# A trunk step on one core: bias gather issued one head ahead, small fills on DVE, the last modulation rows drained two chunks sooner

## The chip, the core and the metric

The kernel runs on one core of a Trainium2 chip. The metric is the time of one execution in device microseconds; the time before is the median of three runs. Engines are named as in the profile: PE (matmuls; PEld its weight loads), DVE (vector), ACT (scalar), POOL (GpSimd), SP (issues most DMAs). All instructions of an engine run in their order, and a DMA that an engine issues stands in that order too.

## What is computed

One layer of a flow-matching trunk on 128 context tokens and 256 latent tokens, width 2048, in fp32. Per layer (cut from the reference):

```python
mod = silu(cond) @ w_mod + b_mod               # six vectors: sh1, sc1, g1, sh2, sc2, g2
h = rmsnorm(x, ln1_g) * (1 + sc1) + sh1
z = h @ w_in                                   # q, k, v, conv a, conv g, LRU x, LRU gate
att = softmax(q k^T * scale + na_bias) v       # 8 heads; window bias for latent tokens, cached context
cv  = silu(layernorm(dwconv31(a * sigmoid(g))))
rec = RG_LRU(dwconv4(x)) * gelu(gate)          # forward and backward scan
x = x + g1 * (concat(att, cv, rec) @ w_out)
h = rmsnorm(x, ln2_g) * (1 + sc2) + sh2
u = dwconv3(h @ ffn_up); ug, uv = split(u)
x = x + g2 * ((silu(ug) * uv) @ ffn_down)
y = rmsnorm(x, final_g)
```

Outputs are y for both token groups, the new keys and values of the context, and the last LRU states.

## The kernel before

Every large product is made of three passes over reduced-width halves (`mm3`, lines L164 to L166: high by high, high by low, low by high). Weights come from HBM by SP's DMAs into `raw`; ACT makes the high half `whi` (L151), DVE the low half `wlo` (L153). All 384 tokens (three row tiles of 128) pass through in one go.

The program runs through the stages: modulation of the first norm, `in_proj` (columns of conv and LRU), `qkv`, `out_proj`, `ffn`. While PE works through the large products of a stage, smaller work is woven in as generators ("streams"): after a number of products `st.turn` advances each stream by some of its yields, and the scheduler fixes each engine's order when the kernel is built. `st.drain(name)` runs what is left of a stream. The streams here are
- `recurrent` (L760 on): per chunk c of four, `lu` is filled with zeros on POOL (L768), then convolved; the two gates, the tails between the token groups set to zero on POOL (L807, L808), the state copied in on POOL (L811), the scans on DVE (L812, L815).
- `conv_module` (L714 on): `cu` filled on POOL (L719), and 31 DVE instructions per chunk (L723, L726) into `cacc`.
- `attention(h)` (L649 on) for each head: after `yield LAG0` it takes two bias tiles and calls `bias_tile`, which loads each in two DMAs on POOL's queue (L643) and masks each half with two selects on POOL (L645, L646). Then three score tiles: PE `S` (L665), DVE adds the bias and takes the maximum (L669 to L674), ACT exponentiates (L675), DVE takes the reciprocal (L676), ACT scales (L677). Then PE transposes the scaled scores into `PTp` (L686) and multiplies them by V (`o`, L695).
- `mods` and `modsd`: the modulation of the second half. Rows of `w_mod` (`rawm`) are loaded by SP for PE's own sums (L383, `modp`), or by POOL (L398) for sums on DVE (L405, L407 into `acc`), which PE gathers with `sel` (L413). `mod_cols` copies the result to M on ACT (L421), PE transposes M (`modt`, L424), DVE adds the bias into MC (L429).

`out_proj` makes five column chunks, `WO_COLS`, of 512, 512, 512, 256 and 256 columns; after each, the residual and its squares (L891, L894, L895) are made for each row tile. After the last chunk `mods` and `modsd` are drained, and the FFN begins with the scaled x (`xs`, L1039), its transposes (`xtp`, L483), `ht` on ACT (L489), `hh` and `hl` on DVE (L491, L492).

Of the kernel before, what the change touches and what calls it, by code (L numbers as in the profile page):

```python
# [18 lines left out]
NH = 8  # L19
# [6 lines left out]
CTX = 128  # L26
# [37 lines left out]
def flat_ap(ap, offset, dims):  # L64
    return bass.AP(tensor=ap.tensor, offset=ap.offset + offset, ap=dims)
# [35 lines left out]
class Trunk:  # L101
# [314 lines left out]
    def mod_cols(self, vec, slot, ln_g, rows):  # L416
        nc = self.nc
        pm = self.aux_ps("modp")
        yield from rows(vec, pm)
        M = self.misc("M")[:, :512]  # L420
        nc.scalar.copy(M, pm)  # L421
        pt = self.aux_ps("modt")
        for b in range(4):
            nc.tensor.transpose(out=pt[:, b * P:(b + 1) * P], in_=M[:, b * P:(b + 1) * P], identity=self.ident)  # L424
        for b in range(4):
            src = pt[:, b * P:(b + 1) * P].rearrange("p (j c) -> p j c", j=4)[:, :, 0:2]
            dst = self.MC[:, slot, b:KT:4, :]
            bm = self.bmod[:, vec * KT + b:(vec + 1) * KT:4]
            nc.vector.tensor_tensor(dst, src, bm.unsqueeze(2).broadcast_to([P, 4, 2]), ALU.add)  # L429
        if ln_g is not None:  # L430
            dst = self.MC[:, slot]
            nc.vector.scalar_tensor_tensor(dst, dst, 1.0, ln_g.unsqueeze(2).broadcast_to([P, KT, 2]), ALU.add, ALU.mult)
# [154 lines left out]
    def qkv(self):  # L587
        nc = self.nc
        h = self.h
        st = self.streams  # L590
        nc.gpsimd.dma_start(self.V[:, 3, :], self.I["cache_v"])

        def v(n):
            pv = [self.mm_ps() for _ in range(3)]
# [37 lines left out]
        qk(6)  # L632


    def bias_tile(self, h):
        nc = self.nc
        bts = [self.slot(LAT, "bias") for _ in range(2)]
        nb = self.I["na_bias"]
        for i in range(2):
            for r in range(2):  # L640
                v = bts[i][r * 64:(r + 1) * 64, :LAT].rearrange("p (k c) -> p k c", c=64)
                off = 3719 - (h * 465 + (10 - (2 * i + r)) * 31 + 15 + 63)
                nc.gpsimd.dma_start(v, flat_ap(nb, off, [[1, 64], [31, 4], [1, 64]]))  # L643
                lo, hi = v[:, :, 16:64], v[:, :, 0:48]
                nc.gpsimd.affine_select(lo, lo, [[0, 4], [-1, 48]], ALU.is_ge, NEG, base=55, channel_multiplier=-1)  # L645
                nc.gpsimd.affine_select(hi, hi, [[0, 4], [1, 48]], ALU.is_ge, NEG, base=-56, channel_multiplier=1)  # L646
        return bts

    def attention(self, h):  # L649
        nc = self.nc  # L650
        q, k = self.z[h], self.z[8 + h]
        yield LAG0
        bt = self.bias_tile(h)
        hs = slice(h * P, (h + 1) * P)
        PT = self.misc("PT")[:, :3 * LAT].rearrange("p (j q) -> p j q", j=3)
        PC = self.slot(P, "PC")
# [1 line left out]
        for i in range(3):  # L658
# [18 lines left out]
            nc.scalar.activation(s, s, AF.Copy, scale=st[:, 2:3])  # L677
            ss.append(s)
            yield 1.0
        yield LAG1  # L680
        for i in range(3):
            n = P if i == 0 else T
# [25 lines left out]
    def conv_module(self):  # L708
# [7 lines left out]
        for c in range(4):  # L716
            a, g = self.z[24 + c], self.z[28 + c]
            u = self.mp.tile([P, W], F32, tag="cu", bufs=2, name="cu")
            nc.gpsimd.memset(u, 0.0)  # L719
            nc.vector.tensor_tensor(u[:, 15:15 + CTX], a[:, :CTX], g[:, :CTX], ALU.mult)  # L720
            nc.vector.tensor_tensor(u[:, 30 + CTX:30 + T], a[:, CTX:], g[:, CTX:], ALU.mult)
            acc = self.slot(N, "cacc")
            nc.vector.tensor_scalar(acc, u[:, 0:N], self.cvw[:, c:c + 1], self.cv_b[:, c:c + 1], ALU.mult, ALU.add)  # L723
            yield 1.0
            for w in range(1, 31):
                nc.vector.scalar_tensor_tensor(acc, u[:, w:w + N], self.cvw[:, 4 * w + c:4 * w + c + 1], acc,  # L726
                                               ALU.mult, ALU.add)
                yield 0.5
            self.mark = nc.vector.tensor_copy(self.cmark, acc[:, 0:1])
            us.append(acc)  # L730
# [29 lines left out]
    def recurrent(self):  # L760
# [4 lines left out]
        for c in range(4):  # L765
            x = self.z[32 + c]
            u = self.mp.tile([P, TP + 3], F32, tag="cu", bufs=2, name="lu")
            nc.gpsimd.memset(u, 0.0)  # L768
            nc.scalar.copy(u[:, 2:2 + CTX], x[:, :CTX])
            nc.scalar.copy(u[:, 4 + CTX:4 + T], x[:, CTX:])  # L770
            xc = self.slot(TP, "xc")
# [30 lines left out]
            for d in range(2):  # L802
# [1 line left out]
                a, gi, r = av[d], gis[d], rs[d]  # L804
                nc.vector.scalar_tensor_tensor(r, a, 1.0, r, ALU.add, ALU.mult)
                nc.vector.tensor_tensor(gi, gi, r, ALU.mult)
                nc.gpsimd.memset(a[:, CTX:CTX + 2], 0.0)  # L807
                nc.gpsimd.memset(gi[:, CTX:CTX + 2], 0.0)  # L808
                st = self.st[:, m:m + 1]
                if d == 0:  # L810
                    nc.gpsimd.tensor_copy(gi[:, CTX + 1:CTX + 2], st)  # L811
                    nc.vector.tensor_tensor_scan(r, a, gi, 0.0, ALU.mult, ALU.add)  # L812
                    nc.vector.tensor_copy(lasts[:, m:m + 1], r[:, CTX - 1:CTX])
                else:
# [24 lines left out]
    def out_proj(self):  # L839
# [32 lines left out]
        for n, (c0, cw) in enumerate(WO_COLS):  # L872
            if n == nn - 1:
                self.ahead = [self.wchunk_slots(self.I["ffn_up"], 0, 4, b, 256) for b in (0, DFF)]
            if n == 0:
                pps = products((0, 1))
            elif n > 1:
                pps = products((n,))
# [17 lines left out]
            if n < 2:  # L896
                with tc.issue_after(ins.ins):
                    self.late_cols(GX, 1024 + n * 512)
        st.drain("mods")
        st.drain("modsd")  # L900
        return ssq

    def late_cols(self, G, c0, cw=512):
# [186 lines left out]
                yield 1.0  # L1090

    def run(self):
        self.mixf, self.gd = {}, {}
        self.setup()
        self.in_proj()
        st = self.streams
# [61 lines left out]
```

## Time and profile before

| | |
|---|---|
| median of three runs | 1807.93 us (1806.61 to 1808.3) |
| the profiled execution | 1806.54 us |
| its span | 1804.6 us |
| its mean granted clock of PE | 0.991 |
| PE busy | 1747.1 us, 97% of the span |
| DVE, ACT, POOL busy | 1158.5, 695.2, 144.9 us |

The profile's page gives each engine's busy time, the chain of work that ended last, and the costliest groups of instructions. The trace behind it answers for any stretch: the timeline of one engine (with the idle time before an instruction and what ended it, in brackets), the waits summed by kind, and busy time with the granted clock by window. All times are microseconds from the start of the span.

### The profile page before, as it was taken

To read this page: it belongs to the slowest core of one execution; us is meant where nothing else is said; L and a number is where in the kernel's file an instruction comes from. 1 tells how busy PE (TensorE), PEld (TensorE's weight loads), DVE (VectorE), ACT (ScalarE), POOL (GpSimd) and SP (SyncE) were. 2 spreads that over 40 slices of the span, in tenths; PEclk is the share of its full clock that TensorE was granted. 3 is DMA by queue.
4 is the path that set the end of the run, shared out by engine and by line. 5 is a ranking of instruction groups with operands and counts; after the bars stand their busy time and mean duration, and the time that the engine had idled before them with its cause. 6 is when DMAs were issued, how large, how long until landed. Compare 5 with 4: busy or idle time off the path is not lost.

```text
span 1804.6 us, 25289 instructions
## 1 busy us (share of the span) xinstructions
PE 1747.1 (97%) x9989; PEld 1579.2 (88%) x9989; DVE 1158.5 (64%) x1629; ACT 695.2 (39%) x1003; POOL 144.9 (8%) x279
## 2 busy tenths in 40 slices
PE   6999998898999999999999999999999999999998
PEld 5789986767987789998989999998989999898987
DVE  4599697795865976449654545449854545448467
ACT  5223455575444335334333333232323333233324
POOL 0100001112441110001000000001000000000002
PEclk9999999999999999999999999999999999999999
DMA  9988659788774864337534343437434343643432
GB/s 335 331 284 284 222 179 260 211 254 240 204 177 157 327 231 138 122 129 246 163 117 131 126 129 117 129 128 225 154 123 129 121 127 116 221 152 121 125 126 108
DMA packets 234551, 325.58 MB, mean 180 GB/s; under 512 B 12140, under 2 KB 169812, under 8 KB 233536
## 3 DMA queue, kind: packets, MB, share of 16 engines
q1 hardware_dynamic: 220976, 277.98, 47.2%
q0 software_dynamic: 13344, 45.94, 9.8%
q8 instruction: 78, 1.28, 0.3%
q14 instruction: 41, 0.34, 0.1%
q10 hardware_dynamic: 112, 0.05, 0.0%
HBM read 316.54 MB, written 7.38 MB: 179 GB/s over the span
## 4 chain that ended last, share of the span: by engine, by line
PE 84%; DVE 7%; DMA 4%; issue 2%; SPq 1%; ACT 1%; POOL 1%; DVEq 0%; POOLq 0%; ACTq 0%
PE mmp L166 26%; PE mmp L165 26%; PE mmp L164 26%; DVE cacc L726 2%; DVE wlo L153 2%; DMA bias<-na_bias 1%; DMA raw<-w_in 1%; DMA rawm<-w_mod 1%; SPq L285 1%; PE modp L295 1%; PE modp L329 0%; PE xtp L483 0%; PE o L695 0%; PE modp L413 0%; PE PTp L686 0%
## 5 line engine op out<-in xcount | busy, mean ns | idle before, releaser
L153 DVE TENSOR_TENSOR wlo<-raw,whi 128x1024 fp32r<-128x1024 f32 x371 | 450.5, 1219 | 360.2 <-ACT whi L151 358.9
L164 PE MATMUL mmp<-hh,whi 128*128 128x386 f32 (+1 forms) x1904 | 649.6, 342 | 3.7 <-DVE z L565 2.9
L166 PE MATMUL mmp<-hh,wlo 128*128 128x386 f32 (+1 forms) x1904 | 650.3, 342 | 0.1
L165 PE MATMUL mmp<-hl,whi 128*128 128x386 f32 (+1 forms) x1904 | 648.4, 341 | 0.1
L151 ACT CAST whi<-raw 128x1024 fp32r<-128x1024 f32 x371 | 387.1, 1045 | 670.3 <-PE mmp L165 380.5
L164 PEld LDWEIGHTS mmp<-hh,whi 128*128 128x128 f32 x1904 | 361.7, 190 | 11.9 <-DVE z L565 4.9
L166 PEld LDWEIGHTS mmp<-hh,wlo 128*128 128x128 f32 x1904 | 360.5, 189 | 5.5 <-issue 4.0
L165 PEld LDWEIGHTS mmp<-hl,whi 128*128 128x128 f32 x1904 | 361.2, 190 | 4.2 <-issue 2.8
L166 PE MATMUL mmp<-whi,gl 128*128 128x512 f32 x504 | 199.2, 395 | 0.0
L165 PE MATMUL mmp<-wlo,gh 128*128 128x512 f32 x504 | 198.8, 394 | 0.1
L164 PE MATMUL mmp<-whi,gh 128*128 128x512 f32 x504 | 198.7, 395 | 0.0
L407 DVE SCALAR_TENSOR_TENSOR acc<-rawm,cT,acc 128x1024 f32<-128x1024 f32 x120 | 150.0, 1284 | 15.7 <-DMA rawm<-w_mod 15.7
L165 PEld LDWEIGHTS mmp<-wlo,gh 128*128 128x128 f32 x504 | 94.9, 188 | 23.1 <-DVE wlo L153 1.0
L164 PEld LDWEIGHTS mmp<-whi,gh 128*128 128x128 f32 x504 | 94.8, 188 | 22.5 <-ACT cv L921 0.8
L166 PEld LDWEIGHTS mmp<-whi,gl 128*128 128x128 f32 x504 | 94.8, 188 | 22.3
L922 DVE SCALAR_TENSOR_TENSOR cv<-mmp,fcw,cv 128x385 f32<-128x385 f32 x88 | 54.0, 616 | 91.7 <-ACT cv L921 91.7
L921 ACT ACTIVATE cv<-mmp,fcb,fcw 128x386 f32<-128x386 f32 x88 | 59.1, 674 | 121.1 <-PE mmp L166 121.1
L1053 DVE TENSOR_TENSOR Y<-mmp,Y 128x512 f32<-128x512 f32 x96 | 65.8, 687 | 40.2 <-PE mmp L166 38.4
L398 POOL DMA_DIRECT2D rawm<-w_mod x64 | 34.9, 546 | 628.0 <-PE modp L413 345.0
L726 DVE SCALAR_TENSOR_TENSOR cacc<-cu,cvw,cacc 128x399 f32<-128x399 f32 x120 | 75.6, 634 | 2.4
L565 DVE TENSOR_TENSOR z<-mmp,z 128x384 f32<-128x384 f32 x100 | 53.4, 553 | 29.9 <-PE mmp L166 29.7
L923 DVE SCALAR_TENSOR_TENSOR cv<-mmp,fcw,cv 128x385 f32<-128x385 f32 x88 | 54.1, 618 | 2.1
(475 smaller groups left out, 1621.8 us busy)
## 6 DMA issues: line engine op xcount, KB each, us to landing
raw<-ffn_up SPq DMA_DIRECT2D x176, 512.0 KB, 3.5
raw<-ffn_down SPq DMA_DIRECT2D x84, 512.0 KB, 3.5
raw<-w_in SPq DMA_DIRECT2D x72, 512.0 KB, 5.4
rawm<-w_mod SPq DMA_DIRECT2D x128, 256.0 KB, 5.8
rawm<-w_mod SPq DMA_DIRECT2D x64, 512.0 KB, 7.1
rawm<-w_mod POOLq DMA_DIRECT2D x64, 512.0 KB, 5.6
raw<-w_out SPq DMA_DIRECT2D x32, 512.0 KB, 5.2
raw<-w_in SPq DMA_DIRECT2D x14, 256.0 KB, 5.1
```

Source lines behind the costliest of these rows:

```text
L151: nc.scalar.copy(hi, raw)
L153: nc.vector.tensor_tensor(lo, raw, hi.bitcast(F32), ALU.subtract)
L164: mm(out, lhsT=a[0], rhs=b[0], start=start, stop=False)
L165: mm(out, lhsT=a[0], rhs=b[1], start=False, stop=False)
L166: mm(out, lhsT=a[1], rhs=b[0], start=False, stop=stop)
L407: nc.vector.scalar_tensor_tensor(acc[c], raws[m], col, acc[c], ALU.mult, ALU.add)
L565: self.mark = nc.vector.tensor_tensor(self.z[f], pz[:, :T], self.z[f], ALU.add)
L726: nc.vector.scalar_tensor_tensor(acc, u[:, w:w + N], self.cvw[:, 4 * w + c:4 * w + c + 1], acc, ALU.mult, ALU.add)
L921: nc.scalar.activation(t, p[:, :TP], AF.Identity, bias=self.fcb[:, f:f + 1], scale=w[1])
L922: nc.vector.scalar_tensor_tensor(t[:, 1:], p[:, 0:TP - 1], w[0], t[:, 1:], ALU.mult, ALU.add)
L923: nc.vector.scalar_tensor_tensor(t[:, :TP - 1], p[:, 1:TP], w[2], t[:, :TP - 1], ALU.mult, ALU.add)
L1053: nc.vector.tensor_tensor(y, p, y, ALU.add)
```

## The change

Four edits. `mod_cols` yields once between the copy to M and the transposes. `bias_tile` is split: `bias_load(h)` takes the two tiles and issues the four DMAs, and `bias_mask(h)` does the eight selects; head 0 is loaded at the start of `qkv`, head h + 1 after the three score tiles of head h, and the masks stand at the start of `attention(h)`, ahead of its first yield. The fills of `cu` and `lu`, the two small ones and the copy of the state go from POOL to DVE (28 instructions in all). In `out_proj` the drains of `mods` and `modsd` stand before the chunk n = 3, not behind n = 4.

```diff
@@ mod_cols
         nc.scalar.copy(M, pm)
+        yield LAG1
         pt = self.aux_ps("modt")
@@ qkv
         nc.gpsimd.dma_start(self.V[:, 3, :], self.I["cache_v"])
+        self.bias_load(0)
@@ attention and its bias
-    def bias_tile(self, h):
-        nc = self.nc
+    def bias_load(self, h):
+
         bts = [self.slot(LAT, "bias") for _ in range(2)]
-        nb = self.I["na_bias"]
         for i in range(2):
             for r in range(2):
                 v = bts[i][r * 64:(r + 1) * 64, :LAT].rearrange("p (k c) -> p k c", c=64)
                 off = 3719 - (h * 465 + (10 - (2 * i + r)) * 31 + 15 + 63)
-                nc.gpsimd.dma_start(v, flat_ap(nb, off, [[1, 64], [31, 4], [1, 64]]))
+                self.nc.gpsimd.dma_start(v, flat_ap(self.I["na_bias"], off, [[1, 64], [31, 4], [1, 64]]))
+        self.bias[h] = bts
+
+    def bias_mask(self, h):
+        nc = self.nc
+        for bt in self.bias[h]:
+            for r in range(2):
+                v = bt[r * 64:(r + 1) * 64, :LAT].rearrange("p (k c) -> p k c", c=64)
                 lo, hi = v[:, :, 16:64], v[:, :, 0:48]
                 nc.gpsimd.affine_select(lo, lo, [[0, 4], [-1, 48]], ALU.is_ge, NEG, base=55, channel_multiplier=-1)
                 nc.gpsimd.affine_select(hi, hi, [[0, 4], [1, 48]], ALU.is_ge, NEG, base=-56, channel_multiplier=1)
-        return bts
+        return self.bias.pop(h)
...
         q, k = self.z[h], self.z[8 + h]
+        bt = self.bias_mask(h)
         yield LAG0
-        bt = self.bias_tile(h)
...
             ss.append(s)
             yield 1.0
+        if h + 1 < NH:
+            self.bias_load(h + 1)
         yield LAG1
@@ conv_module, recurrent
-            nc.gpsimd.memset(u, 0.0)
+            nc.vector.memset(u, 0.0)
...
-                nc.gpsimd.memset(a[:, CTX:CTX + 2], 0.0)
-                nc.gpsimd.memset(gi[:, CTX:CTX + 2], 0.0)
+                nc.vector.memset(a[:, CTX:CTX + 2], 0.0)
+                nc.vector.memset(gi[:, CTX:CTX + 2], 0.0)
                 st = self.st[:, m:m + 1]
                 if d == 0:
-                    nc.gpsimd.tensor_copy(gi[:, CTX + 1:CTX + 2], st)
+                    nc.vector.tensor_copy(gi[:, CTX + 1:CTX + 2], st)
@@ out_proj
             if n == nn - 1:
                 self.ahead = [self.wchunk_slots(self.I["ffn_up"], 0, 4, b, 256) for b in (0, DFF)]
+            if n == nn - 2:
+                st.drain("mods")
+                st.drain("modsd")
...
-        st.drain("mods")
-        st.drain("modsd")
         return ssq
```

The scheduler gives each engine a new order from this. Three places follow. POOL, in `qkv`, around the loads of the bias of heads 0 and 1, before; V is the tile in which a scan's inputs lie, `bias_3042` and `bias_3043` are the two tiles of head 0:

```order
L768 MEMSET lu_3275 128x389
L643 DMA bias_3042<-na_bias 64x4x64 x2
L643 DMA bias_3043<-na_bias 64x4x64 x2
L645 AFFINE_SELECT bias_3042<-bias_3042 64x4x48
...
L807 MEMSET V_2522 128x2
L645 AFFINE_SELECT bias_3043<-bias_3043 64x4x48
L646 AFFINE_SELECT bias_3043<-bias_3043 64x4x48
L808 MEMSET V_2522 128x2
L811 COPY V_2522<-pcol_81 128x1
```

And now, where `bias_2524` and `bias_2525` are those of head 0, and `bias_3201` and `bias_3202` those of head 1:

```order
L592 DMA V_2522<-cache_v 128x1024
L644 DMA bias_2524<-na_bias 64x4x64 x2
L644 DMA bias_2525<-na_bias 64x4x64 x2
L653 AFFINE_SELECT bias_2524<-bias_2524 64x4x48
...
L654 AFFINE_SELECT bias_2525<-bias_2525 64x4x48
L644 DMA bias_3201<-na_bias 64x4x64 x2
L644 DMA bias_3202<-na_bias 64x4x64 x2
...
L654 AFFINE_SELECT bias_3202<-bias_3202 64x4x48
L449 DMA gate2_3437<-M_3435 2x512 x4
```

The fills and the copy are gone from between the masks, and each head's loads and masks stand one head earlier. POOL again, at the third row of DVE's modulation sums in head 3, before (`rawm_4323`; `bias_4174` is head 3's second tile):

```order
L643 DMA bias_4173<-na_bias 64x4x64 x2
L643 DMA bias_4174<-na_bias 64x4x64 x2
...
L628 DMA out_new_v<-V_2522 128x1024
L645 AFFINE_SELECT bias_4174<-bias_4174 64x4x48 x2
L646 AFFINE_SELECT bias_4174<-bias_4174 64x4x48 x2
L398 DMA rawm_4323<-w_mod 128x1024
L398 DMA rawm_4399<-w_mod 128x1024
L398 DMA rawm_4432<-w_mod 128x1024
```

And now, where that row is `rawm_4329`, and `bias_4317` and `bias_4318` are the tiles of head 4:

```order
L398 DMA rawm_4284<-w_mod 128x1024
L630 DMA out_new_v<-V_2522 128x1024
L398 DMA rawm_4329<-w_mod 128x1024
L644 DMA bias_4317<-na_bias 64x4x64 x2
L644 DMA bias_4318<-na_bias 64x4x64 x2
...
L653 AFFINE_SELECT bias_4318<-bias_4318 64x4x48
L654 AFFINE_SELECT bias_4318<-bias_4318 64x4x48
L398 DMA rawm_4395<-w_mod 128x1024
L398 DMA rawm_4438<-w_mod 128x1024
```

The third row moved ahead of the loads, and the fourth and fifth moved behind six masks of the next head. PE, at the end of `out_proj` before, from the last product of the last chunk (`mmp_6196`) to the first of the FFN (`mmp_6631`); `xs_6398`, `xs_6400`, `xs_6402` are the three row tiles:

```order
L166 MATMUL mmp_6196<-whi_6289,mix7l_5603 128x256
L413 MATMUL modp_4214<-acc_5440,sel_88 32x512
L413 MATMUL modp_4214<-acc_5441,sel_88 32x512
...
L424 MATMUL modt_6380<-ident_72,M_6378 128x128
L483 MATMUL xtp_6404<-ident_72,xs_6398 128x128
L483 MATMUL xtp_6404<-ident_72,xs_6400 128x128
...
L424 MATMUL modt_6380<-ident_72,M_6378 128x128 x3
L483 MATMUL xtp_6428<-ident_72,xs_6398 128x128
...
L164 MATMUL mmp_6631<-hh_6409,wsh_6160 128x386
```

And now, the L413 within the products of the chunk n = 3 (`mmp_5994` is its second row tile, `mmp_5995` its third), then, in the chunk n = 4 (`mmp_6210`, `mmp_6211`), the transposes of x:

```order
L165 MATMUL mmp_5994<-wlo_6083,mix10h_5408 128x256
L413 MATMUL modp_4214<-acc_5440,sel_88 32x512
L166 MATMUL mmp_5994<-whi_6082,mix10l_5409 128x256
...
L413 MATMUL modp_4214<-acc_5441,sel_88 32x512
...
L425 MATMUL modt_5984<-ident_72,M_5982 128x128 x4
L164 MATMUL mmp_5995<-whi_6082,mix9h_5404 128x256
...
L164 MATMUL mmp_6210<-whi_6304,mix6h_5598 128x256
L484 MATMUL xtp_6404<-ident_72,xs_6398 128x128
...
L484 MATMUL xtp_6404<-ident_72,xs_6400 128x128
...
L484 MATMUL xtp_6404<-ident_72,xs_6402 128x128
```

The four L413, the four transposes of M and those of the first two row tiles left the tail and stand between products.

## Rows read from the trace of the kernel before

**Rows 1.** The page's part 1: busy us, share of the span and instructions by engine.

```profile
PE 1747.1 (97%) x9989; PEld 1579.2 (88%) x9989; DVE 1158.5 (64%) x1629; ACT 695.2 (39%) x1003; POOL 144.9 (8%) x279
```

**Rows 2.** Waits of PE, grouped: us in total, times, longest.

```profile
PE PTp L686 <- ACT s L677: 20.2, 6, 10.6
```

**Rows 3.** Timeline of PE: start us, duration us, instruction [idle before <- what ended it].

```profile
318.01 0.48 PE L686 MATMUL PTp<-ident,s 128*128 128x128 f32 x1 [10.55 <-ACT s L677]
...
361.33 0.48 PE L686 MATMUL PTp<-ident,s 128*128 128x128 f32 x1 [5.68 <-ACT s L677]
...
444.47 0.95 PE L424 MATMUL modt<-ident,M 128*128 128x128 f32 x4 [4.32 <-ACT M L421]
...
488.50 0.33 PE L686 MATMUL PTp<-ident,s 128*128 128x128 f32 x1 [1.77 <-ACT s L677]
...
589.29 0.50 PE L165 MATMUL mmp<-wlo,mix6h 128*128 128x512 f32 x1 [2.67 <-DVE wlo L153]
```

**Rows 4.** Timeline of POOL, the fill ahead of head 0's bias loads.

```profile
294.32 0.42 POOL L768 MEMSET lu<- 128x389 f32 x1 [21.45 <-DVE cacc L726]
```

**Rows 5.** The chain that ended last: start us, us, piece of the chain.

```profile
296.56 13.94 DMA bias<-na_bias
...
346.88 11.33 DMA bias<-na_bias
...
434.90 5.33 DMA rawm<-w_mod
```

**Rows 6.** Timeline of DVE, the scan behind POOL's copy.

```profile
308.30 0.96 DVE L812 TENSOR_TENSOR_SCAN V<-V 128x386 f32<-128x386 f32 x1 [9.02 <-POOL V L811]
```

**Rows 7.** Windows: start:end, length, busy by engine (instructions), PEclk, DMA share, GB/s.

```profile
318.00:322.30 4.30, 4.29 (x17) 4.26 (x17) 4.30 (x12) 3.17 (x8) 0.00 (x0) 0.56 0.21 59
...
361.30:366.00 4.70, 4.67 (x11) 3.25 (x11) 4.44 (x9) 2.69 (x5) 1.15 (x4) 0.50 0.48 153
...
444.40:450.00 5.60, 4.79 (x17) 4.39 (x18) 4.36 (x12) 3.16 (x7) 0.53 (x1) 0.53 0.65 189
...
589.20:595.00 5.80, 5.71 (x25) 4.68 (x26) 5.80 (x8) 0.33 (x1) 2.54 (x4) 1.00 1.03 392
```

**Rows 8.** Windows of 10 us from 255 to 405, one of them, and the sum.

```profile
275.00:285.00 10.00, 10.00 (x67) 7.17 (x66) 9.68 (x16) 3.38 (x3) 0.00 (x0) 1.00 1.01 329
...
sum 150.00, PE 131.82 PEld 100.80 DVE 121.48 ACT 94.64 POOL 24.56; mean PE 8.79 PEld 6.72 DVE 8.10 ACT 6.31 POOL 1.64
```

**Rows 9.** Groups of DVE by line and form: busy us, mean ns, idle before.

```profile
L205 DVE MEMSET ones<- 128x128 f32 x1 | 0.2, 165 | 0.8 <-PEq L1151 0.8
```

**Rows 10.** Timeline of PE from the third chunk to the FFN.

```profile
641.53 0.29 PE L166 MATMUL mmp<-whi,mix10l 128*128 128x256 f32 x1
...
663.32 1.92 PE L413 MATMUL modp<-acc,sel 128*32 128x512 f32 x8
...
667.81 0.52 PE L483 MATMUL xtp<-ident,xs 128*128 128x128 f32 x3 [0.57 <-DVE MC L429]
668.91 0.97 PE L164 MATMUL mmp<-hh,wsh 128*128 128x386 f32 x4 [0.58 <-DVE hh L491]
```

**Rows 11.** Timeline of DVE there.

```profile
641.42 1.28 DVE L407 SCALAR_TENSOR_TENSOR acc<-rawm,cT,acc 128x1024 f32<-128x1024 f32 x1
...
657.78 0.42 DVE L891 TENSOR_TENSOR G<-mmp,G 128x256 f32<-128x256 f32 x1 [4.66 <-PE mmp L166]
...
660.16 0.42 DVE L1039 TENSOR_SCALAR xs<-X,rstd 128x384 f32<-128x384 f32 x1 [0.76 <-POOL rstd L474]
660.60 0.43 DVE L891 TENSOR_TENSOR mmp<-mmp,G 128x256 f32<-128x256 f32 x1
```

**Rows 12.** Timeline of POOL, masks of heads 0 and 4.

```profile
302.00 0.35 POOL L646 TENSOR_SCALAR_AFFINE_SELECT bias<-bias 64x192 f32<-64x192 f32 x1
...
477.33 1.22 POOL L646 TENSOR_SCALAR_AFFINE_SELECT bias<-bias 64x192 f32<-64x192 f32 x1
```

**Rows 13.** Timeline of DVE beside the masks of head 4.

```profile
481.94 1.37 DVE L407 SCALAR_TENSOR_TENSOR acc<-rawm,cT,acc 128x1024 f32<-128x1024 f32 x1
```

More of the change, by code (lines that the diff above doesn't have):

```diff
@@ L767, in recurrent @@
             u = self.mp.tile([P, TP + 3], F32, tag="cu", bufs=2, name="lu")
-            nc.gpsimd.memset(u, 0.0)
+            nc.vector.memset(u, 0.0)
             nc.scalar.copy(u[:, 2:2 + CTX], x[:, :CTX])
@@ L1092, in run @@
     def run(self):
-        self.mixf, self.gd = {}, {}
+        self.mixf, self.gd, self.bias = {}, {}, {}
         self.setup()
```

## The prediction

> **What bounds the kernel now.** I read the page's busy shares first: PE is busy for 97% of the span [rows 1], so only PE's idle stretches, and the stretches in which its clock is low, can be given back. Next the waits of PE, grouped: the transposes of the softmaxed scores, `PTp` (L686), wait six times on ACT's scaling of a score tile (L677), 20.2 us in all [rows 2]. Then PE's timeline around the long ones: 10.55 us before 318.01 (head 0), 5.68 before 361.33 (head 1), 4.32 before 444.47 (head 3, `modt` behind M), 1.77 before 488.50 (head 4), 2.67 before 589.29 (a late wlo) [rows 3]. After about 700 us PE hardly waits, and what lies before 120 us is not touched. So the change is decided between 290 and 700 us.
>
> Why PE waits is read backwards from the chain and from POOL. POOL works in order. Its fill of `lu` (L768) waits 21.45 us for the convolution's DVE work, until 294.32 [rows 4], and the bias loads of head 0 stand behind it. The chain has one of them from 296.56 for 13.94 us, one of head 1 from 346.88 for 11.33 [rows 5]. The masks wait for the loads, and the small fills and the copy L811 stand between and behind the masks, so the scan on DVE is held 9.02 us for L811, until 308.30 [rows 6]. Everything that DVE has queued behind that scan, the reciprocals of head 0 included, is then caught up while PE stands still. In head 3 a modulation row `rawm` on POOL's queue is issued behind bias masks, at 434.90, and takes 5.33 us [rows 5]; DVE, ACT and PE follow it to 444.47 [rows 3].
>
> The three long waits cost twice, since PE comes back at the lower of its two clock levels, 1.2 in place of 2.4 GHz: granted 0.56 over 318.0 to 322.3, 0.50 over 361.3 to 366.0, 0.53 over 444.4 to 450.0. After the wait of 2.67 us it stayed at 1.00 [rows 7].
>
> **Part by part: bias loads and masks a head ahead.** By the order, head 0's loads and masks run in the projection stage with nothing near that needs them; head 1's loads take the place of head 0's (waits that end at 285 to 295 on the scale of before), head 2's follow at the old place of head 1's. A load takes up to 13.94 us [rows 5], and a head is 43.3 us behind the one before it (318.01 to 361.33 [rows 3]), some 35 without the gaps, so loads and masks have about 20 us of cover. Nothing is added to the masks' number (8 a head). With the loads gone from there, the scan no longer waits on POOL, and the next thing that is late is DVE's own work.
> - Head 0: 10.55 of wait, and 4.3 x (1 - 0.56) = 1.9 of clock [rows 3, 7], together 12.4. I walk DVE's queue from 296 on by its own durations: the first reciprocal ends about 308.1, ACT's scaling 308.4, and PE wants the tile near 307.6. I leave 0.9 of wait, and no clock loss since 1.77 and 2.67 brought none. Gain 11.5 (bounds 9 and 12.4).
> - Head 1: 5.68, and 4.7 x (1 - 0.50) = 2.3; the same walk puts the first reciprocal 3 us ahead of PE and the next about level. Leave 0.4: gain 7.6 (6 to 8).
> - Head 3: in the order, the third `rawm` now stands ahead of head 4's loads and waits only for V's copy and for the product chunk before it, about 429 against 434.90; its 5.33 us then end at 434.4 in place of 440.2 [rows 5]. The diff's new yield also moves `modt` behind the score transposes. 4.32, and 5.6 x (1 - 0.53) = 2.6 less 0.4 for a short wait inside that stretch [rows 3, 7]; leave 0.4. Gain 6.1 (4 to 6.5). The next two `rawm` now stand behind masks of head 4, up to 3.5 us later than before; the walk shows that DVE reaches their sums in about the same time, and that the weight splits behind them have 8 us of lead. I take nothing for that (0 to 2).
> - Head 4 and the short waits of `PTp`: the six hold 20.2, the three named 18.0 [rows 2, 3], so 2.2 are left in three others. I credit 1.2 of these and 0.7 of head 4's 1.77: 1.9 (0 to 4).
> - The 2.67 us at 589.29 stay: its `rawm` stands on POOL behind the loads of X, and the change leaves these.
> Together 11.5 + 7.6 + 6.1 + 1.9 = 27.1.
>
> **Fills on DVE.** 28 instructions leave POOL: 4 of 429 columns, 4 of 389, 16 of 2, 4 copies of one column. A DVE fill of 128 columns took 165 ns [rows 9], and one of 389 on POOL 0.42 us [rows 4]; I take 0.4 for a large one and 0.1 for a small one: 8 x 0.4 + 20 x 0.1 = 5.2 us (bounds 2.5 and 6.5), the first two at the program's start, where they are free. Where does the rest hide? From 255 to 405 DVE is busy 121.5 us, and PE 131.8, of which about 4 are its low clock [rows 8], so DVE has 121.5 + 3.5 (three of the four chunks) = 125 of work in the 127.8 that are left once the gaps go. That is 98%. In 275 to 285 DVE was busy 9.68 of 10.00 and PE still 10.00 [rows 8], so such a load is borne, but the cover is thin: I charge 2.0 for collisions (0 to 8).
>
> A row and a rule go against this cover. A mask took 0.35 us at 302.00, with DVE idle, and 1.22 at 477.33, with DVE at work [rows 12]; the DVE sum beside the latter took 1.37 at 481.94 [rows 13] against 1.28 at 641.42 [rows 11]. The masks of heads 1 to 3 now fall into full DVE time: 24 x 0.09 = 2.2 us of DVE, inside the 2.0 with its bounds. The Trainium skill ("SBUF — State Buffer", section "Who interferes with whom") says that a VectorE instruction with two SBUF inputs contends with a GpSimd instruction that reads SBUF, and not with one that only writes it, and calls the shared ports an exclusive lock. By its second half the fills never disturbed DVE on POOL, so to move them relieves DVE of nothing; the rows show no sign against that. By the lock, DVE would lose what a mask takes; the 0.09 says otherwise, and this is a rival below.
>
> **Last modulation rows drained sooner.** The order puts the first L413 of these rows into the second row tile of the chunk n=3, ahead of the product that PE began at 641.53 [rows 10], and its DVE sum (L407) ended only at 641.42 + 1.28 = 642.70 [rows 11]: a new wait of 1.2. The last four L413 (1.92 for 8, so 0.95) and four transposes (0.45) lay in the tail, where PE waited anyway, and now stand in the stream, with 0.15 for M: 2.75 in all. Behind it, the transposes of x (`xtp`) of the first two row tiles move from the tail into the products of n=4. A row tile's xs is ready 2.80 us after its last product (657.78 to 660.16 + 0.42 [rows 11]), and the order puts its transposes behind 19 or 20 products of the next; 24 products take 660.60 - 657.78 = 2.82 [rows 11], so PE gets there after 2.3: waits of 0.5 and 0.4, and 0.3 of transposes each, 1.5. The tail from the last product to the first FFN product was 668.91 - 663.32 = 5.6 [rows 10]; now it is 2.8 for xs and, as from 667.81 to 668.91 [rows 10], 1.1 and a bit: 4.1. So 2.75 + 1.5 - 1.5 = a cost of 2.8 (bounds 0.5, if the waits vanish, and 4.5).
>
> **Sum.** 27.1 - 2.0 - 2.8 = 22.3. The profiled run took 1806.5, so 1784.2; it stands 1.4 under the median of the runs, so the median becomes about 1785.6.
>
> **Rivals.**
> (A) DVE takes the place of the bias. With 98% to do, whatever is badly placed comes late at the heads' reciprocals. Heads 0 and 1 would then wait some 3 to 3.5 us each, and fall to the low clock again (2 us each): about 10.5 in place of 1.3, and 1785.6 + 9 = 1795. For it: under 3 us of room in 150, and a queue in order. Against: PE ran at 10.00 beside a DVE at 9.68 [rows 8].
> (B) The walk is too dark: neither leftovers (1.3) nor collisions (2.0) nor the waits in the drain (2.1) come: 1785.6 - 5.4 = 1780.
> (C) The bias is no longer last but DVE pays for the masks: the lock costs DVE 1.22 - 0.35 = 0.87 a mask, 24 masks, 21 us, near 1804.5, no measurable change. It is the page's rule named above; the 0.09 of the row speaks against it.
> (D) Slower: the drain catches up what the heads gave. Were the modulation rows tied to transfers and not to PE, the last sum would still end at 642.70, and PE would reach the first L413 27 us sooner, at 614. It would wait 28.3, lose 2 to the clock, and pay the other 1.6 of the drain: 1806.5 - 27.1 + 28.3 + 2 + 1.6 = 1811.3, on the median 1812.7. It decides only if the rows come on hardly any sooner than before; each microsecond by which they follow PE is taken off. Against: the `rawm` ahead of the 2.67 us wait stood behind a load that is released by PE's own work, so the stream moves with PE.
> (E) The loads are issued no sooner, as the slots that they fill come free only then: the time stays near 1807, with 1 to 3 us of fills. The order names no such wait for heads 0 to 2.
>
> **Chances.** The forecast 0.53, (A) 0.25, (B) 0.12, (C) 0.03, (D) 0.04, (E) 0.03. A measurement of this kernel can tell 0.2%, or 3.6 us, from no change: faster holds the forecast, (A) and (B), 0.90; same (C) and (E), 0.06; slower (D), 0.04. The range runs from (B) to just above (A), 1780 to 1796; the forecast's own is 1782 to 1790.
>
> **What would show it.** Right: PE's waits of `PTp` on L677 fall from 20.2 to under 4; no wait of DVE on POOL's bias or L811 between 295 and 365; the granted clock stays 1.00 from 300 to 460; a new wait of PE before L413 of about 1 us, and a shorter tail before FFN. Wrong: PTp waits of 3 us and more with the clock at 0.5 behind them (A), waits of L413 over 5 us (D), DVE's two-input work longer by far beside masks (C), or a wait of the bias loads that ends where it did (E).

## The result and the profile after

| | before | after |
|---|---|---|
| median of the runs side by side | 1808.12 us | 1783.57 us (1781.7 to 1784.68) |
| ratio, with its 95% interval | | 0.9862 [0.9844, 0.9879] |
| span of the profiled run | 1804.6 us | 1782.3 us |
| its mean granted clock of PE | 0.991 | 0.995 |

The kernel is 1.4% faster, and the time lies 2.0 us below the forecast of 1785.6. That is closer than the working deserves: two of its terms were off by some 5 to 7 us each, in opposite directions, and that these errors cancel is luck.

Part 1 of the page after, against [rows 1]: POOL has 28 instructions fewer, DVE 28 more for 2.2 us.

```profile
PE 1743.9 (98%) x9989; PEld 1576.3 (88%) x9989; DVE 1160.7 (65%) x1657; ACT 695.2 (39%) x1003; POOL 140.6 (8%) x251
```

The waits of PE after, grouped (us in total, times, longest), against [rows 2]. The 20.2 us of the softmaxed tiles are 0.9 now. Lines are left out at the marks, the longest of them `modp` (L295) at the program's start, which has 11.9 here and 10.9 before. Of what lies behind the start, three waits of `xtp` at the end of `out_proj` lead, and they are new.

```profile
PE xtp L484 <- DVE xs L1050: 4.0, 3, 2.9
...
PE mmp L165 <- DVE wlo L153: 2.5, 1, 2.5
...
PE modp L413 <- DVE acc L407: 1.3, 1, 1.3
PE PTp L696 <- ACT s L685: 0.9, 2, 0.6
```

**Where the time went.** Both kernels run the same products in nearly the same order, so the n-th product of L164 can be compared in the two traces. Its start, after minus before, worked out from the two timelines:

```
product n   start before   after - before
      360      278.8           +1.88     (what lies before has shifted as a whole; other runs stand up to 2.3 us off either way)
      420      344.3          -10.37     head 0
      480      421.6          -19.82     heads 1 and 2
      540      470.2          -27.76     head 3
      600      509.2          -30.03     head 4
      780      639.2          -28.88
      840      660.4          -22.81     the drain
      900      701.9          -21.20
     2760     1778.5          -22.05
```

From n=360 to 600 the change gains 31.9 us, up to 780 it gives 1.15 back, and from 780 to 900 it loses 7.7.

The windows of these four stretches, before (start:end, length, then busy us and instructions of PE, PEld, DVE, ACT, POOL, then granted clock, DMA share, GB/s):

```profile
278.80:344.30 65.50, 54.95 (x388) 45.07 (x387) 50.91 (x92) 39.27 (x56) 8.74 (x23) 0.92 0.75 212
344.30:421.60 77.30, 69.67 (x445) 50.31 (x444) 53.13 (x101) 47.56 (x72) 17.89 (x42) 0.96 0.90 258
421.60:470.20 48.60, 43.53 (x279) 40.03 (x278) 32.07 (x43) 23.85 (x39) 13.22 (x25) 0.93 0.75 216
470.20:509.20 39.00, 37.23 (x216) 36.04 (x215) 34.50 (x45) 16.55 (x32) 21.54 (x29) 1.00 0.91 199
```

The same stretches after, in the same columns:

```profile
280.70:333.90 53.20, 53.20 (x387) 43.25 (x386) 51.05 (x99) 39.05 (x56) 9.65 (x18) 1.00 0.90 262
333.90:401.80 67.90, 67.34 (x445) 49.01 (x444) 54.51 (x113) 47.25 (x72) 13.41 (x23) 1.00 0.99 293
401.80:442.40 40.60, 40.60 (x278) 37.38 (x277) 32.80 (x44) 23.87 (x39) 13.44 (x24) 1.00 0.86 258
442.40:479.20 36.80, 36.80 (x218) 36.33 (x216) 28.75 (x36) 15.36 (x28) 14.89 (x23) 1.00 0.80 192
```

Length less PE's busy time is its idle time: 10.55 + 7.63 + 5.07 + 1.77 = 25.0 us before, 0.56 after. PE's busy time falls from 205.4 to 197.9 for the same products, 7.4 us, as the granted clock goes from 0.92 to 0.96 to 1.00 throughout. So nearly all of the waits and all of the low clock are gone: 24.5 + 7.4 = 31.9.

POOL's timeline after, against [rows 4, 12]: head 1's loads are issued at 279.01 and 296.35, a head sooner. The third row of DVE's sums no longer stands behind a head's masks; it is issued at 408.35.

```profile
279.01 1.24 POOL L644 DMA_DIRECT2D bias<-na_bias  x2 [65.07 <-DVE cu L731]
...
296.35 1.22 POOL L644 DMA_DIRECT2D bias<-na_bias  x2 [16.11 <-PE mmp L166]
...
307.03 0.58 POOL L654 TENSOR_SCALAR_AFFINE_SELECT bias<-bias 64x192 f32<-64x192 f32 x1
...
342.78 1.23 POOL L654 TENSOR_SCALAR_AFFINE_SELECT bias<-bias 64x192 f32<-64x192 f32 x1
...
408.35 0.55 POOL L398 DMA_DIRECT2D rawm<-w_mod  x1 [4.03 <-DMA raw<-w_in]
```

DVE's timeline, against [rows 6, 11]: a convolution instruction beside two masks takes 0.71 us, the scan has no wait in brackets any more, head 0's reciprocal ends at 309.01, and the last sum of the modulation at 612.77 + 1.28 = 614.05.

```profile
302.15 0.95 DVE L822 TENSOR_TENSOR_SCAN V<-V 128x386 f32<-128x386 f32 x1
...
306.67 0.71 DVE L736 SCALAR_TENSOR_TENSOR cacc<-cu,cvw,cacc 128x399 f32<-128x399 f32 x1
...
308.86 0.15 DVE L684 RECIPROCAL st<-st 128x1 f32<-128x1 f32 x1
...
612.77 1.28 DVE L407 SCALAR_TENSOR_TENSOR acc<-rawm,cT,acc 128x1024 f32<-128x1024 f32 x1
```

PE's timeline, against [rows 3, 10]: the first `PTp` of head 0 comes without a wait. In the drain, eight records of L413 stand in the stream, 1.29 us of wait ahead of them, then M's transposes, then three waits of `xtp`.

```profile
309.54 0.29 PE L696 MATMUL PTp<-ident,s 128*128 128x128 f32 x1
...
614.10 1.05 PE L413 MATMUL modp<-acc,sel 128*32 128x512 f32 x2 [1.29 <-DVE acc L407]
615.08 0.38 PE L166 MATMUL mmp<-whi,mix10l 128*128 128x256 f32 x1
...
616.80 1.91 PE L413 MATMUL modp<-acc,sel 128*32 128x512 f32 x6
618.64 0.39 PE L164 MATMUL mmp<-whi,mix7h 128*128 128x256 f32 x1
...
636.62 0.55 PE L484 MATMUL xtp<-ident,xs 128*128 128x128 f32 x3 [0.59 <-DVE xs L1050]
...
640.62 0.55 PE L484 MATMUL xtp<-ident,xs 128*128 128x128 f32 x3 [0.51 <-DVE xs L1050]
...
641.36 0.28 PE L166 MATMUL mmp<-whi,mix7l 128*128 128x256 f32 x1
644.57 0.90 PE L484 MATMUL xtp<-ident,xs 128*128 128x128 f32 x3 [2.94 <-DVE xs L1050]
...
646.52 1.66 PE L164 MATMUL mmp<-hh,wsh 128*128 128x386 f32 x4 [1.05 <-DVE hh L492]
```

The windows from the tail into the FFN, after (columns as above), show what the list of waits does not: the FFN's first products run at 0.50 of the clock, 1.2 GHz.

```profile
645.00:647.00 2.00, 0.95 (x4) 0.55 (x3) 0.86 (x3) 1.91 (x5) 0.00 (x0) 0.50 0.42 172
647.00:649.00 2.00, 2.00 (x8) 2.00 (x8) 1.97 (x5) 0.62 (x2) 0.00 (x0) 0.50 0.00 0
649.00:651.00 2.00, 2.00 (x8) 2.00 (x7) 2.00 (x3) 0.00 (x0) 0.20 (x2) 0.50 0.33 76
651.00:653.00 2.00, 2.00 (x12) 2.00 (x11) 1.97 (x6) 0.00 (x0) 0.22 (x1) 0.91 0.94 293
```

### The profile page after: what moved, and what is told of

It is laid out like the page before. It is cut to its first block, busy times and chain, and to the rows that moved or that the text cites. A ratio compares the mean times of both kernels' runs of the same rounds, so it can differ in the third digit from the quotient of the medians.

```text
span 1782.3 us, 25275 instructions
## 1 busy us (share of the span) xinstructions
PE 1743.9 (98%) x9989; PEld 1576.3 (88%) x9989; DVE 1160.7 (65%) x1657; ACT 695.2 (39%) x1003; POOL 140.6 (8%) x251
## 3 DMA queue, kind: packets, MB, share of 16 engines
q8 instruction: 78, 1.28, 0.3%
## 4 chain that ended last, share of the span: by engine, by line
PE 89%; DMA 3%; DVE 2%; issue 2%; SPq 2%; POOL 1%; ACT 1%; DVEq 0%; POOLq 0%; ACTq 0%
PE mmp L166 28%; PE mmp L164 28%; PE mmp L165 27%; DMA rawm<-w_mod 2%; PE modp L383 2%; SPq L285 1%; DVE wlo L153 1%; DVE acc L407 1%; PE modp L295 1%; PE o L705 1%; PE modp L329 1%; PE modp L413 0%; PE xtp L484 0%; DMA raw<-ffn_up 0%; DMA raw<-w_in 0%
## 5 line engine op out<-in xcount | busy, mean ns | idle before, releaser
L164 PE MATMUL mmp<-hh,whi 128*128 128x386 f32 (+1 forms) x1904 | 648.6, 341 | 3.7 <-DVE z L566 2.9
L164 PEld LDWEIGHTS mmp<-hh,whi 128*128 128x128 f32 x1904 | 360.6, 189 | 12.0 <-DVE z L566 4.9
L164 PE MATMUL mmp<-whi,gh 128*128 128x512 f32 x504 | 198.9, 395 | 0.0
L407 DVE SCALAR_TENSOR_TENSOR acc<-rawm,cT,acc 128x1024 f32<-128x1024 f32 x120 | 149.1, 1281 | 16.6 <-DMA rawm<-w_mod 16.6
L164 PEld LDWEIGHTS mmp<-whi,gh 128*128 128x128 f32 x504 | 94.9, 188 | 22.7 <-ACT cv L932 0.8
```

The costliest lines, as they stand in the source:

```text
L164: mm(out, lhsT=a[0], rhs=b[0], start=start, stop=False)
L407: nc.vector.scalar_tensor_tensor(acc[c], raws[m], col, acc[c], ALU.mult, ALU.add)
```

## The experiments

The theory after the result: (T1) the heads lost their time to what stands ahead of something urgent in POOL's queue, and the early loads remove that; (T2) the early drain costs some 8 us, because it takes from the tail the small PE work that had run there for nothing and had kept the clock up. The rivals are named with each run. Times are medians. The ratio is to the kernel before in runs on the same chip, whose own median was 1804.9 to 1808.9 from batch to batch, so ratios are compared.

| run | us | ratio [95%] |
|---|---|---|
| after | 1783.57 | 0.9862 [0.9844, 0.9879] |
| e1_drain_late | 1777.44 | 0.9841 [0.9827, 0.9856] |
| e2_bias_only | 1792.63 | 0.9923 [0.9907, 0.9940] |
| e3_fills_only | 1788.22 | 0.9899 [0.9884, 0.9914] |
| e4_drain_only | 1813.74 | 1.0045 [1.0030, 1.0060] |
| e5_large_fills | 1791.40 | 0.9902 [0.9886, 0.9919] |
| e6_small_fills | 1790.07 | 0.9910 [0.9892, 0.9927] |
| e7_drain_one_sooner | 1781.60 | 0.9851 [0.9836, 0.9865] |
| e9_no_yield | 1777.32 | 0.9826 [0.9812, 0.9841] |
| e8_rows_ahead | 1776.03 | 0.9821 [0.9806, 0.9835] |
| e10_store_on_act | 1772.91 | 0.9817 [0.9802, 0.9832] |

### The drain put back, and the drain alone

e1_drain_late is the kernel after without the last edit; e4_drain_only is the kernel before with that edit alone.

```diff
 # e1_drain_late, against after (e4_drain_only: the reverse, against before)
-            if n == nn - 2:
-                st.drain("mods")
-                st.drain("modsd")
...
+        st.drain("mods")
+        st.drain("modsd")
         return ssq
```

> The changed kernel with its fourth part undone: mods and modsd are drained behind the last chunk again. My theory: the early drain costs 7.7 us (PE's lead over the kernel before shrinks from 28.9 us ahead of the first L413 to 21.2 after the first FFN products), by work that lay in the tail, new waits and a low clock at the FFN's start; so this kernel takes 1776 (1774 to 1779), and the clock stays at 1.00 behind the tail. Rival, that the early drain pays (the tail before FFN is shorter and the rest is an unlucky run): 1783 to 1787.

> The kernel before with the early drain, nothing else. My theory: the drain's cost does not depend on the rest: 7.7 us more, 1816 (1813 to 1819), with a wait before L413 of 1 to 1.5 us, a tail wait of about 3 us for xs, and a granted clock of 0.5 behind it. Rival, that it costs only where PE comes 29 us sooner to the last modulation rows: at most 3 us, 1808 to 1811.

Both times lie in the expected ranges, on both sides of the kernel before: 1777.44 and 1813.74. The tail of e1 keeps the clock. Its PE timeline has the eight L413 in the tail and a wait of 0.58 before the FFN, as [rows 10]:

```profile
632.55 1.92 PE L413 MATMUL modp<-acc,sel 128*32 128x512 f32 x8
...
638.14 0.97 PE L164 MATMUL mmp<-hh,wsh 128*128 128x386 f32 x4 [0.58 <-DVE hh L492]
```

and the clock of e1 there stands at 1.00, as this window of its tail shows:

```profile
636.00:638.00 2.00, 0.99 (x8) 0.55 (x6) 0.65 (x5) 1.29 (x4) 2.00 (x7) 1.00 0.86 248
```

The waits of PE in e4 have the same `xtp` and nearly none of L413, so the expected 1 to 1.5 us before L413 did not come:

```profile
PE xtp L483 <- DVE xs L1040: 4.0, 3, 2.9
...
PE modp L413 <- DVE acc L407: 0.2, 1, 0.2
```

A window of e4 behind its tail stands at the lower clock again:

```profile
676.00:678.00 2.00, 2.00 (x7) 2.00 (x8) 1.97 (x4) 0.86 (x3) 0.00 (x0) 0.50 0.00 0
```

So the clock is lost with the drain alone and kept without it. Of all twelve traces, the three with an early drain (after, e4, e7) have the lower clock behind this tail, and the nine others stand at 1.00. The size is less sharp than the sign. The traces put 7.7 us between the products 780 and 900 of after and 5.7 of e4; by the ratios the drain costs 0.21% in after against e1 (3.8 us, and their intervals overlap) and 0.45% in e4 (8 us). 4 to 8 us is what can be said.

Part of this spread is not the drain's. The wait for `wlo` in `out_proj` (2.67 us in before, 2.56 in e4) left the clock at 1.00 in the trace of before and lowered it in that of e4. The windows around it, before and then e4:

```profile
580.00:600.00 20.00, 17.33 (x75) 13.78 (x74) 14.21 (x16) 4.59 (x5) 9.48 (x16) 1.00 1.02 380
580.00:600.00 20.00, 17.44 (x69) 13.68 (x68) 12.78 (x14) 4.20 (x4) 9.57 (x16) 0.91 1.01 380
```

That is 20 x 0.09 = 1.8 us of full clock. e4 loses them against before, which makes the drain look dearer there; e1 loses about as much behind its wait of 2.27 us, and after nothing behind 2.54, which makes the drain look cheaper in after against e1.

### The drain one chunk sooner

```diff
 # e7_drain_one_sooner, against after
-            if n == nn - 2:
+            if n == nn - 1:
                 st.drain("mods")
                 st.drain("modsd")
```

> The changed kernel with mods and modsd drained before the last chunk (n = 4) in place of n = 3. PE then finds the last modulation sums done, so the wait of 1.3 us before L413 goes; the L413 and transposes in the stream, the transposes of x among the products, the idle tail and the low clock behind it stay. My theory: 1782.3 (1781 to 1784), that is 6 of the drain's 6 to 8 us are displaced work, the tail and the clock. Rival, that the wait for the rows is what it costs: 1778 to 1779.

This gives the sums one chunk more, and the wait before L413 is gone, as expected; the three waits of `xtp` (4.0 us) and the lower clock remain. The window of e7:

```profile
645.00:647.00 2.00, 2.00 (x8) 2.00 (x7) 1.97 (x4) 0.54 (x2) 0.00 (x0) 0.50 0.00 0
```

It loses 5.1 us between the products 780 and 900 and stands 4.3 us above e9 in the same batch. The wait before L413 was thus the smaller part of the drain's price: of the 2.6 us between after and e7 in this stretch it is 1.3.

### The bias alone

The split and the early loads are in, the fills stay on POOL, the drain stays late, the yield is out.

```diff
 # e2_bias_only, against after (drain late and yield out, besides)
-            nc.vector.memset(u, 0.0)
+            nc.gpsimd.memset(u, 0.0)
...
-                nc.vector.memset(a[:, CTX:CTX + 2], 0.0)
-                nc.vector.memset(gi[:, CTX:CTX + 2], 0.0)
+                nc.gpsimd.memset(a[:, CTX:CTX + 2], 0.0)
+                nc.gpsimd.memset(gi[:, CTX:CTX + 2], 0.0)
...
-                    nc.vector.tensor_copy(gi[:, CTX + 1:CTX + 2], st)
+                    nc.gpsimd.tensor_copy(gi[:, CTX + 1:CTX + 2], st)
```

> The kernel before with the bias split and issued a head ahead, nothing else: fills on POOL, no yield, drain at the end. My theory: the bias was most of it, but fills still stand behind masks of the next head, so a scan is held some 3 us and head 0 keeps a wait of 2 to 4 us: 1780 (1777 to 1786), against 1776 for all but the drain. Rival, that bias and fills are needed together, since the scan waits for POOL as before: 1790 or more. Rival, that the fills are nothing but load for DVE: the same as the kernel with the late drain, or 1 to 2 us under it.

T1 in this form failed, and the rival held: 1792.63, not 1780. PE waits as much as half of before:

```profile
PE PTp L695 <- ACT s L684: 10.9, 4, 5.0
```

DVE's timeline of e2 has scans held for a small fill, 4.94 us in this one and 3.90 in another:

```profile
311.58 1.02 DVE L824 TENSOR_TENSOR_SCAN V<-a,pcol,V 128x386 f32<-128x386 f32 x1 [4.94 <-POOL V L817]
```

and POOL's timeline shows why: the fill, 0.09 us of work, stands behind the masks of the next head, and those behind their loads.

```profile
311.15 0.35 POOL L653 TENSOR_SCALAR_AFFINE_SELECT bias<-bias 64x192 f32<-64x192 f32 x1
311.46 0.09 POOL L817 MEMSET V<- 128x2 f32 x1
```

The early masks meet the fills of the recurrence in POOL's queue; the bias moved a head ahead alone brings the old hold back, one head later.

### The fills alone, all of them and each set by itself

```diff
 # e3_fills_only: all 28, against before; e5_large_fills: the first line, twice (8 instructions);
 # e6_small_fills: the others (20 instructions)
-            nc.gpsimd.memset(u, 0.0)
+            nc.vector.memset(u, 0.0)
...
-                nc.gpsimd.memset(a[:, CTX:CTX + 2], 0.0)
-                nc.gpsimd.memset(gi[:, CTX:CTX + 2], 0.0)
+                nc.vector.memset(a[:, CTX:CTX + 2], 0.0)
+                nc.vector.memset(gi[:, CTX:CTX + 2], 0.0)
...
-                    nc.gpsimd.tensor_copy(gi[:, CTX + 1:CTX + 2], st)
+                    nc.vector.tensor_copy(gi[:, CTX + 1:CTX + 2], st)
```

> The kernel before with the 28 fills on DVE, nothing else. By its order head 0's bias loads no longer stand behind a fill that waits for the convolution, so they are issued some 40 us earlier with no split at all; head 1's still stand behind the gate's DMAs (M, about 327 us), head 3's modulation row still behind masks. My theory: the queue position is the cause, not the distance of a head: head 0's wait goes (12 us), head 1's mostly (4 to 7), head 3's stays: 1791 (1787 to 1796). Rival, that the loads must be a head ahead: under 5 us gained, 1803 or more.

> The kernel before with only the eight large fills (cu, lu) on DVE; the twenty small ones stay on POOL. By the order the loads of head 0 then stand behind the small fills of an earlier chunk, not behind the fill that waited 21 us, and the copy for the scan stands behind masks that are done by then. My theory, that the one large fill with its wait held the queue: nearly what all 28 gave, 1790 (1787 to 1794; all 28 gave 1788). Rival, that the scan waiting for its copy behind the masks is the cause: little is gained, 1800 or more.

> The kernel before with only the twenty small fills on DVE; the eight large ones stay on POOL. By the order the loads of head 0 now stand ahead of the fill of lu that waits for the convolution (with the small fills gone from the queue the loads move up), and seven of the eight masks right behind that fill. My theory, that what counts is which instructions stand ahead of the loads and masks and not which fills are slow: the masks end near 298 us, the scan waits for nothing on POOL, and the gain is that of the large fills alone, 1790 (1787 to 1795, by ratio 0.988 to 0.993). Rival, that the large fill's wait of 21 us is the cause: it is still there, so 1800 or more.

All three came as expected. The fills alone bring 18 us, more than the bias alone (13). In e3 the waits of `PTp` are nearly gone without any load moved by the code: the first of head 0's are issued at 231.76, since the fill that waited for the convolution no longer stands ahead of them. (Their own wait, 41.84 us, ends on DVE's L721, long before head 0 needs them.) POOL's timeline of e3 (at 414.98 a row of the modulation behind a head's masks):

```profile
231.76 1.26 POOL L643 DMA_DIRECT2D bias<-na_bias  x2 [41.84 <-DVE cu L721]
...
414.98 0.60 POOL L398 DMA_DIRECT2D rawm<-w_mod  x1
```

What stays in e3 is head 3, which the row at 414.98 sets; its PE timeline:

```profile
424.66 1.03 PE L424 MATMUL modt<-ident,M 128*128 128x128 f32 x4 [3.67 <-ACT M L421]
```

With either set moved alone most of the gain is there. In e5 the copy L811 follows at 300.96, and scan and reciprocals with it; in e6 the order that the scheduler made has head 0's loads ahead of the fill of `lu`, at 276.98 against 296.56, so its wait of 12.25 us holds no load. POOL's timeline of e5:

```profile
269.72 2.51 POOL L643 DMA_DIRECT2D bias<-na_bias  x4
...
300.96 0.18 POOL L811 COPY V<-pcol 128x1 f32<-128x1 f32 x1
```

POOL's timeline of e6:

```profile
276.98 2.49 POOL L643 DMA_DIRECT2D bias<-na_bias  x4
...
296.56 0.42 POOL L768 MEMSET lu<- 128x389 f32 x1 [12.25 <-DVE cacc L726]
```

PE still waits 7.1 us for `PTp` in e5 and 5.0 in e6 (six and five waits, none over 3.2). So the price was the order of one queue, not the work in it. The large fills and the small ones remove the same hold at two ends, and the two sums (17.5 and 14.8 us) do not add.

### The yield

```diff
 # e9_no_yield, against e1_drain_late
         nc.scalar.copy(M, pm)
-        yield LAG1
         pt = self.aux_ps("modt")
```

> The late drain, and the yield between M and its transposes taken out again. With the yield M is ready at 415.7 us, 0.5 us before PE would reach the transposes without it. My theory: the gain of head 3 comes from the modulation row ahead of the bias loads on POOL, so nothing changes: 1777.4 (1776 to 1779). Rival, that the yield hides M: PE waits 2 us or more in head 3 again, 1780 to 1783.

1777.32 against 1777.44 for e1, with overlapping intervals of the ratios: the yield has no effect that can be measured. Head 3 gains 8.0 us in e9 (products 480 to 540) as it does in after (7.9) and in e2, which has no yield either (8.2), and nothing in e3, where the modulation's row still stands behind the masks: head 3's gain is that this row now stands ahead of the loads of head 4 [rows 5].

### The wait that the change left, in two steps

The last long wait of before [rows 3] remains in after, 2.5 us, and its row stands on POOL behind the loads of X. e8 puts those loads behind the last row that the sums of this stage need; e10 takes one more DMA off POOL's queue.

```diff
 # e8_rows_ahead, against e1_drain_late: rl is the last rawm load issued by then
-                for cc in (0, 512):
-                    self.late_cols(G, cc)
+                with tc.issue_after(rl.ins):
+                    for cc in (0, 512):
+                        self.late_cols(G, cc)
...
-                with tc.issue_after(ins.ins):
+                with tc.issue_after(rl.ins):
                     self.late_cols(GX, 1024 + n * 512)
 # e10_store_on_act: this, besides
-            nc.gpsimd.dma_start(self.O["new_k"][:, (h - 3) * P:(h + 1) * P], kk)
+            nc.scalar.dma_start(self.O["new_k"][:, (h - 3) * P:(h + 1) * P], kk)
```

> The late drain, and the loads of X for the residual put behind the modulation rows on POOL's queue (the first of them waits 29 us for the last head's product, with a row behind it, and makes the wait of 2.3 us for wlo near 555). My theory: that wait goes and nothing takes its place: 1775.1 (1774 to 1776.5) against 1777.4 with the late drain alone. Rival, that X then comes late for the residual, or that transfers collide: 1777 to 1780.

> The late drain, the modulation rows ahead of X on POOL's queue, and the store of the new keys issued by ACT, which has just made them, so that it no longer holds the rows behind it on POOL (25 us of wait at 546.8 in the run without this). My theory: the wait for wlo near 556, 1.3 us there, goes: 1774.7 (1773 to 1776; 1.2 us under the run without, by ratio 0.9814). Rival, that the next rows wait for the sums on DVE anyway or that ACT's queue is held: no change or slower, 1776 to 1778.

e8 did half of it. Its wait before the product is 1.27 (PE's timeline):

```profile
557.10 0.51 PE L165 MATMUL mmp<-wlo,mix6h 128*128 128x512 f32 x1 [1.27 <-DVE wlo L153]
```

since the next thing in POOL's queue now holds the rows, the store of the new keys, which waits 24.91 us for ACT (POOL's timeline):

```profile
546.76 0.55 POOL L715 DMA_DIRECT2D out_new_k<-kk  x1 [24.91 <-ACT kk L714]
```

Its time, 1.3 us under e9 in the same batch, lies inside the intervals of both. In e10 ACT, which makes `kk`, issues that store itself, and no wait for `wlo` is left between 285 and 690. e10 is the best version here: 1772.91, ratio 0.9817 [0.9802, 0.9832]. Against after (0.9862) it stands clear; against e1 (0.9841), e8 (0.9821) and e9 (0.9826) the intervals overlap, and what the two steps bring beyond the late drain is seen in the traces (between the products 360 and 780 e10 gains 34.1 us on before, e9 29.8), not settled by the times. Of these 4.3 us, 2.4 are the wait itself, and some 1.7 are the clock, which e9 has at 0.98 and 0.94 in the two windows of 20 us from 540 on and e8 and e10 keep at 1.00.

## Why the prediction was right, and where it was not

**The sign, the place and the mechanism: right.** All gain lies between 279 and 510, in the waits of `PTp` and `modt` and the low clock behind them; the other waits on the list were called as they came: the one before L413 (1.29, forecast 1.2), the first two of `xtp` (0.59 and 0.51, forecast 0.5 and 0.4), and the `wlo` wait that stays (2.5).

**Heads 0 to 4, forecast 27.1 less 2.0 for crowding, measured 31.9.** The missing 6.8 has four parts. The leftovers of 0.9, 0.4 and 0.4 did not come: the first reciprocal is done by 309.01, and PE does not wait at 309.54 (+1.7). The charge for crowding was not paid (+2.0): the fills and the copies take 4.7 us of DVE together, close to the 5.2 forecast, and a mask costs a DVE instruction beside it under 0.1 us on average (rival C below), but PE waits for none of it, with 0.56 us idle in the four stretches. The two large fills of DVE by line and form (busy us, mean ns, idle before):

```profile
L729 DVE MEMSET cu<- 128x429 f32 x4 | 1.7, 416 | 0.2
...
L778 DVE MEMSET lu<- 128x389 f32 x4 | 1.5, 383 | 0.1
```

The short waits were under-credited: the windows hold 25.0 us of idle, of which three large waits are 20.55, so 4.5 were to be had, 3.9 went, and 1.9 stood in the sum (+2.0). The low clock cost 7.4 of busy time in these windows, not the 6.4 credited (+1.0). These make 6.7.

**The drain, forecast 2.8, measured 7.7 in the trace (4 to 8 by the times): the step that failed.** Its waits were right; its work and its tail were not. The step took half of the L413 (0.95) as the part that moves. The eight records of [rows 10] are two for each of four instructions, and all eight moved: by the starts around them they take 0.98 + 1.84 = 2.8 us of the stream (+1.85). The tail from the last product's end is 4.9 us (641.36 + 0.28 = 641.64 to 646.52), not 4.1 (+0.8). And a term was not in the sum at all: the small work that left the tail had kept PE going there. In after PE stands 2.94 us in that tail, does three transposes, waits 1.05, and has the lower clock from there to 651: 4.5 x 0.5 + 2 x 0.09 = 2.4 us (+2.4). Against these, a wait of 0.7 for `hh` that before had in the FFN's start is gone. 2.8 + 1.85 + 0.8 + 2.4 - 0.7 = 7.2, near enough to 7.7. The sentence "no clock loss since 1.77 and 2.67 brought none" was not asked again for the new tail. It also rested on one trace: the heads did not test it, as no wait of theirs is over 0.6 us now, and the `wlo` wait that it names, 2.3 to 2.7 us long where it remains whole, left the clock at 1.00 in before and after and was followed by the lower one in the eight other traces that have it (e1 to e7 and e9).

**Rivals.** (A), DVE in the bias's place: fell, PE is busy 53.20 of 53.20 us over head 0 with DVE at 51.05. (B), the walk too dark, held for the heads and not for the drain, which is why its 1780 was not reached; e1, without the drain, reaches it (1777.44; by its ratio 0.9841 x 1808.12 = 1779.4). (C), DVE pays 0.87 us for each mask: fell. A mask went up to 1.23 us beside DVE's work, as before [rows 12], and DVE paid too, but little: the four of 120 convolution instructions that lie beside a mask after took 0.71 us on average, the others 0.63, and the L407 beside masks 1.32 against 1.28. The Trainium skill ("SBUF — State Buffer", section "Who interferes with whom") has an instruction with two SBUF inputs contend with a GpSimd instruction that reads SBUF; these rows agree, with POOL paying up to 0.87 us and DVE under 0.1 on average. (D): the wait before L413 is 1.29 and not 28.3, as the sums came with PE. (E): fell, since head 1's loads are issued at 279.01 and 296.35, a head sooner; they did wait there, 65.07 and 16.11 us, for others to finish, as (E) has it, but early enough.

**What stays open.** What the drain costs by itself is known to 4 to 8 us only, and why the clock fell behind the same `wlo` wait in one trace and not in another is not shown. The 1.15 us lost between products 600 and 780 are not assigned: 0.6 of them is idle time of PE, the rest more busy time for the same products.

## What to carry to other kernels

Before an engine's work is called cheap, see what waits in its queue ahead of the DMAs it issues: 0.09 us fills and a 0.4 us fill held loads, scans and PE for 4 to 21 us, and whatever was cleared, the next waiting entry (masks, then the X loads, then a store) took its place. A tail in which PE waits anyway is a cheap place for small PE work: here it cost nothing there and the clock stayed up, so moving it out to shorten the tail is priced with the whole of the moved work, the new waits in the stream and the clock behind the tail. That a wait of some 2 us left the clock alone in one trace is no promise for the next. And count records against instructions before a group's busy time is split.

## What the runs showed of the hardware that was not expected

- PE's clock fell to its lower level behind the new tail, whose longest wait was 2.94 us with 0.90 us of transposes and 1.05 of wait behind it, in all three kernels that have this tail. Behind the `wlo` wait, with products right after it, it stayed at 1.00 in before (2.67 us) [rows 7] and in after (2.54), and fell in e4 (2.56) and seven others (2.27 to 2.66): nearly the same wait, with either outcome.
- A fill of 389 columns takes 383 ns on DVE and 0.42 us on POOL, one of two columns 0.06 on DVE (timeline) and 0.09 on POOL: the engines hardly differ, and what a fill costs is what stands before and behind it.
- A mask on POOL takes 0.35 us, or up to 1.23 beside DVE's two-input work; of that work, a convolution instruction beside masks took 0.71 us where others took 0.63.
